# Rows of 1,088 instead of 1,056 elements in the weight tiles of a dense transformer block

## The chip, the cores and the metric

The kernel runs on one core of a Trainium2 chip. The metric is the device time of one execution in microseconds (us). Three runs of the kernel before took 1647.96, 1648.25 and 1648.37 us; the median is 1648.25 us.

## The reference

One layer of a streaming encoder on 256 frames of 2,048 features, all in float32:

```
h  = x + W_out( sum_b sigmoid(g_b) * W_branch_b( mixer_b( RMSNorm(x) ) ) )   # gated linear attention, gMLP
h  = h + W_down( relu(W_up RMSNorm(h))^2 )                                    # hidden size 8,192
y  = RMSNorm(h)
```

Nearly all the arithmetic is in products of a [256 x 2048] activation with 2,048 x 512 pieces of weight matrices: the input projection (14,352 columns), the two branch products, the output product, and the two products of the MLP.

## The kernel before

**Products.** `gemm` (line 185) multiplies 256 tokens by 2,048 rows and 512 columns of a weight matrix. It is called 72 times. 71 calls have 512 columns; one, the third, has 528 in two parts of 264. A call goes through its 2,048 rows in 8 blocks (`kb` 0 to 7) of 256 rows, two K-tiles of 128 rows each.

**Precision.** Each float32 operand is split into a high part in the format fp32r and a low part that holds the rest, and a product is made of three matmuls: high by high (line 197), low by high (line 198), high by low (line 199). A block of a call with 512 columns therefore has 2 K-tiles x 2 token tiles x 3 = 12 matmuls, and each has one K-tile of the activation, 128 x 128, as the stationary operand (read by the weight load, LDWEIGHTS) and 512 columns of the weights as the moving operand. So "weight load" in the profile's words reads the activation, and the matrix called weights here streams through. The moving operand of one matmul is 512 elements, 2,048 bytes, of each partition.

**Weight tiles.** `split_weights` (line 170) fetches a block: a load into a raw tile `w` issued on the queue of SyncE (line 178), a ScalarE copy that rounds it to the high part `wh` (line 179), and a VectorE subtraction that makes the low part `wl` (line 180). The three kinds of tile have 5, 4 and 4 buffers, which are taken in turn, one of each for a block. As every call has 8 blocks, the blocks with even `kb` use the buffers 0 and 2 of `wh` and `wl`, and those with odd `kb` the buffers 1 and 3, in every call.

**Activations.** The high and low parts of an activation, and most intermediate results, are in tiles of the pool `slots` (`slot`, 4 K-tiles x 256 tokens, 4,096 bytes of a partition; `pair` has the same size). K-tiles 0 and 1 of such a tile go with even `kb`, K-tiles 2 and 3 with odd `kb`. Smaller tiles `ev` and `bg` are in the pool `work`.

**Order.** The order of the work is the program's own; short steps (transposes, the small products of the mixers) are put between the blocks of the next product (`drain`). TensorE gets block after block without a gap as long as the buffers are filled in time.

**Places in SBUF.** The pools lie one behind the other in each partition: 16,384 bytes of scratch, 128 bytes of constants, the pool of constants and of the residual `h` up to byte 36,736, then the buffers of `w`, `wh` and `wl`, then `slots`, `work` and the small columns. A row of 1,056 float32 elements is 4,224 bytes, or 16.5 x 256; 36,736 is 143.5 x 256. In the built program the buffers begin here:

| tile | first byte of each buffer in a partition | remainder by 256 |
|---|---|---|
| `w` | 36,736, then every 4,224 | 128, 0, 128, 0, 128 |
| `wh` | 57,856, 62,080, 66,304, 70,528 | 0, 128, 0, 128 |
| `wl` | 74,752, 78,976, 83,200, 87,424 | 0, 128, 0, 128 |
| `slot`, `pair` | 91,648, then every 4,096 | 0 |
| `ev` / `bg` | 210,432 / 222,720, then every 2,048 | 0 |
| `h`, `ident` | 16,512, 33,408 | 128 |

A K-tile of a weight block begins 0 or 2,048 bytes into its buffer, and a stationary operand a multiple of 512 bytes into its `slot`, so the remainders are also those of the operands of the matmuls (in the calls with 512 columns).

Of the kernel before, what the change touches and what calls it, by code (L numbers as in the profile page):

```python
# [9 lines left out]
F32 = mybir.dt.float32  # L10
F32R = mybir.dt.float32r
# [24 lines left out]
C_GV = 8208  # L36
C_G = 10256

V_MLP, V_GLA, V_BA, V_BS = 0, 16, 20, 28
NVEC = 36  # L40


class Operand:
    """An activation with features on partitions, as high and low parts: tiles of 4 K-tiles."""

    def __init__(self):
        self.hi, self.lo = [], []
# [8 lines left out]
def block_kernel(  # L56
# [33 lines left out]
    def uid(s):  # L90
        count[0] += 1
        return f"{s}_{count[0]}"
# [2 lines left out]
        return slots.tile([P, 4, T], dt, tag="slot", name=uid("slot"))  # L95

    def pair_tile():
        """[128, 2, 512]: 512 features of both token tiles, tokens on partitions"""
        return slots.tile([P, NTT, CB], F32, tag="slot", name=uid("pair"))

    def flat(t):
# [14 lines left out]
    def cols(j, n=CB):  # L116
        return slice(j * n, (j + 1) * n)

    # As long as `in_order` is set, the steps on the way to the products keep their order.
    in_order = [True]  # L120

    def pin(ins):
        return tc.keep_in_program_order(ins) if in_order[0] else ins

    # Steps that need TensorE for a short time wait here, and run between the K-tiles of the
    # next large product, when what they read is long there.
    pending = deque()

    def drain(n=1):
        for _ in range(min(n, len(pending))):  # L130
            pending.popleft()()

    # ---- x, in blocks of 256 features; constants
    h = cpool.tile([P, NTT, D], F32, name="h")
    xv = x[0].rearrange("(t p) d -> p t d", p=P)

# [2 lines left out]
        nc.sync.dma_start(h[:, :, s], xv[:, :, s])  # L139

    def late(dst, src):
        """A load that must not run ahead of the weights'."""
        tc.keep_in_program_order(nc.scalar.dma_start(dst, src))

    load_x(0)
# [11 lines left out]
    nc.gpsimd.memset(starts.rearrange("p (c s) -> p c s", s=CHUNK)[:, :, 0:1], 0.0)  # L157

    def to_partitions(src, n, name):
        """[n, 128] -> [128, n]"""  # L160
        dst = cpool.tile([P, n], F32, name=name)
        tp = tr_ps()
        nc.tensor.transpose(tp[:, 0:n], src, ident[0:n, 0:n])
        pin(nc.vector.tensor_copy(dst, tp[:, 0:n]))
        return lambda i: dst[:, i : i + 1]

    mix_col = to_partitions(vec_n, KT, "mixw")

    # ---- shared steps
    def split_weights(src, by_k=False):  # L170
        """[128, nk, n] of DRAM -> its high and low parts in SBUF."""
        k, n = src.shape[1], src.shape[1] * src.shape[2]
        w = wpool.tile([P, 2 * 528], F32, tag="w", name=uid("w"), bufs=5)
        hi = wpool.tile([P, 2 * 528], F32R, tag="wh", name=uid("wh"), bufs=4)
        lo = wpool.tile([P, 2 * 528], F32R, tag="wl", name=uid("wl"), bufs=4)
        wv, hv, lv = [t[:, 0:n].rearrange("p (k n) -> p k n", k=k) for t in (w, hi, lo)]
        for s in [slice(i, i + 1) for i in range(k)] if by_k else [slice(0, k)]:
            nc.sync.dma_start(wv[:, s], src[:, s])  # L178
            pin(nc.scalar.copy(hv[:, s], wv[:, s]))  # L179
            pin(nc.vector.tensor_tensor(  # L180
                lv[:, s], wv[:, s], hv[:, s].bitcast(F32), op=ALU.subtract
            ))
        return hv, lv

    def gemm(a, w, c0, n=CB, parts=1, k0=0, after=None, split_tail=False):
        """256 tokens of a @ w[k0 : k0 + 2048, c0 : c0 + n]: PSUM tiles [part][token tile]."""
        ps = [[mm_ps() for _ in range(NTT)] for _ in range(parts)]
        m = n // parts
        held = []

        def products(kt, tt, hi, lo):
            ah, al = a.at(kt, tt)
            for i in range(parts):
                o = ps[i][tt][:, 0:m]
                wh = hi[:, kt % 2, cols(i, m)]
                wl = lo[:, kt % 2, cols(i, m)]
                pin(nc.tensor.matmul(o, lhsT=ah, rhs=wh, start=kt == 0, stop=False))  # L197
                pin(nc.tensor.matmul(o, lhsT=al, rhs=wh, start=False, stop=False))  # L198
                pin(nc.tensor.matmul(o, lhsT=ah, rhs=wl, start=False, stop=kt == KT - 1))  # L199

        for kb in range(KT // 2):
            r0 = k0 + kb * 2 * P
            hi, lo = split_weights(
                w[r0 : r0 + 2 * P, c0 : c0 + n].rearrange("(k p) n -> p k n", p=P),
                by_k=after is not None and kb == 0,
            )
            if after is not None:
                after(kb)
            if kb > 1 or kb == 1 and len(pending) > 6:
                drain()  # L210
            while a.ready < 2 * kb + 2:
                drain()
            if split_tail and kb >= KT // 2 - 3:
                held.append((kb, hi, lo))
                continue
            for kk in range(2):
                for tt in range(NTT):
                    products(2 * kb + kk, tt, hi, lo)
        if held:
            for tt in range(NTT):  # L220
                for kb, hi, lo in held:
                    for kk in range(2):
                        products(2 * kb + kk, tt, hi, lo)
        return ps

    def to_operand_pair(dst, src, scale=None):
        """Two K-tiles of dst from src[token tile] [128, 256], tokens on partitions."""
        kt0 = dst.ready
        if kt0 % 4 == 0:
            dst.hi.append(slot(F32R))  # L230
# [24 lines left out]
        dst.ready += 2  # L255

    def to_operand(dst, src, scale=None):
        """to_operand_pair of four K-tiles; TensorE's way is the shorter one."""
        for half in range(2):
            part = [src[:, tt, cols(half, 2 * P)] for tt in range(NTT)]  # L260
            pending.append(lambda part=part: to_operand_pair(dst, part, scale))

    def transpose_quadrants(dst, src, jm):
        """Rows 32 jm ... of dst [128, 4 K-tiles, 256 tokens], the transpose of a pair."""
        sv = src.rearrange("p t (k m b) -> p m k t b", m=4, b=32)
        dv = dst.rearrange("p k (t i b) -> p i k t b", t=NTT, b=32)
        for i in range(4):
            nc.vector.transpose(dv[cols(jm, 32), i], sv[cols(i, 32), jm])  # L268

    def to_operand_vector(dst, src, scale=None):  # L270
        """to_operand with VectorE's transposes, in blocks of 32."""
        tr = []

        def step(jm):
# [24 lines left out]
        pending.append(split)  # L299

    def rsqrt_of(sums, n, width=1):
        """(sums / n + eps) ** -0.5"""
        m = col(2)[:, 0:width]
        nc.vector.tensor_scalar(m, sums, 1.0 / n, EPS, op0=ALU.mult, op1=ALU.add)  # L304
        r = col(2)[:, 0:width]
        nc.gpsimd.tensor_tensor(r, m, mhalf[:, 0:width], op=ALU.pow)  # L306
        return r
# [12 lines left out]
        return r  # L320

    def scaled(ps, scale, func=AF.Copy):
        """func(ps * scale) of both token tiles, in SBUF."""
        res = pair_tile()
        for tt in range(NTT):
            nc.scalar.activation(res[:, tt, :], ps[tt], func, scale=scale[tt])  # L326
        return res

    # ---- the projection's operand; the rows' scale is applied behind the products
    wi = w_in[0]  # L330
    xT = Operand()
    xsq = [cpool.tile([P, 4], F32, name=f"xsq{tt}") for tt in range(NTT)]
# [12 lines left out]
            x_step(kb + 1)  # L345

    def transposed(ps, scale, into):
        """[256, 512] of the projection, with features on partitions."""
        sb = scaled(ps, scale)

        def step(jm):
# [16 lines left out]
        rstd_q.append(rq)  # L368
    transposed(ps, rstd, kT)

    # ---- constants that are needed later
    vec_m = cpool.tile([NVEC, P], F32, name="vec_m")
    for row, src in ((V_MLP, norm_mlp_w), (V_GLA, gla_norm_w), (V_BA, b_alpha)):
        n = src.shape[1] // P
        late(vec_m[row : row + n, :], src[0].rearrange("(a p) -> a p", p=P))
    late(vec_m[V_BS : V_BS + GROUPS, :], b_spatial[0])
    # w_alpha_up's rows as high, low and high parts, against the gate's high, high and low parts
    wal_in = flat(slot())[0 : 3 * RANK, :]
    for i in range(3):
        late(wal_in[i * RANK : (i + 1) * RANK, :], w_alpha_up[0])  # L380
# [36 lines left out]

        pending.append(step)

    # ---- mixer A: gated linear attention  # L420
    transposed(gemm(xT, wi, C_K + CB)[0], rstd, kT)
    for i in range(2):
        pending.append(lambda i=i: wal_step(i))

    # the last head's r and the gate's low-rank rows, in one product of two parts
    ps = gemm(xT, wi, C_R + 3 * CB, n=CB + RANK, parts=2)
    half = (CB + RANK) // 2
    glrT = cpool.tile([3 * RANK, T], F32R, name="glrT")
# [22 lines left out]

    pending.append(glr_step)

    # decays: features on partitions, tokens along the row
    E, decay, zs = [], [], []

    def z_step(b, pair):
# [12 lines left out]
                z[:, 2 * pair + i, :], zp[:, cols(i, T)], AF.Identity, bias=vcol(V_BA + dt)  # L470
            )

    # log sigmoid(z) = min(z, 0) - ln(1 + exp(-|z|)), and its sums along each chunk
    logs = []

    def log_step(b, func, **args):
        """One function for both halves in a row: a table of functions takes long to load."""
        if func is AF.Abs:
            logs.append(slot())
        src = zs[b] if func is AF.Abs else logs[b]  # L480
# [40 lines left out]
    for b in range(2):  # L521
        transposed(gemm(xT, wi, C_Q + b * CB)[0], rstd_q, qT)

    # scores[s, t] = sum_d q[t, d] k[s, d] exp(L[end of t's chunk, d] - L[s, d]), s on partitions
    S, scaled_qk = [], []

    def scale_step(b):
# [102 lines left out]

        pending.append(gate_step)

    # ---- gated merge of the branches
    mixed = []

    def merge(br, a):
# [20 lines left out]

    merge(0, oT)

    # ---- mixer B: gMLP spatial gating, a block of 128 frames per token tile  # L660
    ln = flat(slot())
    lnw, lnb = ln[:, 0:DG], ln[:, DG : 2 * DG]
    late(lnw, gmlp_ln_w[0].partition_broadcast(P))
# [53 lines left out]

    mT = merge(1, gT)

    # ---- the residual, and the MLP's operand  # L720
    hT = Operand()
    hsq = [cpool.tile([P, 4], F32, name=f"hsq{tt}") for tt in range(NTT)]
    for j in range(4):
# [6 lines left out]
            sum_squares(hsq[tt][:, j : j + 1], part[:, tt])  # L730
    rstd2 = [row_rstd(hsq[tt], f"rstd2{tt}") for tt in range(NTT)]

    # ---- MLP, in four stages of 2048 hidden features; the down product follows one stage behind
    def up(st, j, f):
        ps = gemm(hT, w_ff_up[0], st * D + j * CB)[0]
        a = scaled(ps, rstd2, AF.Relu)
# [22 lines left out]
                if j == 2:  # L759
                    rest.append(mean_square(fsq[tt][:, 0:3]))  # L760

    # ---- the final norm
    rest = []

    def mean_square(parts):
# [74 lines left out]
```

## Time and profile before

| | |
|---|---|
| median of three runs | 1648.25 us |
| span of the profiled execution, first to last instruction | 1647.4 us |
| TensorE (PE) matmul busy | 1630.6 us, 99% |
| weight loads (PEld) busy | 1332.3 us, 81% |
| VectorE (DVE) busy | 1130.2 us, 69% |
| ScalarE (ACT) busy | 753.4 us, 46% |
| DMA engines, mean share | 61% for the queue of the weight loads, 189 GB/s |

Engines: PE is TensorE's matmuls, PEld its weight loads, which run beside the matmuls. The duration shown for a matmul contains its passage through a pipeline, so two matmuls overlap; the distance from one start to the next is what a matmul costs. A number behind L is a line of the kernel.

### The profile page before, as it was taken

Reading aid. Unit: us, or ns where it says so; the run is one execution under the profiler, and the core shown is the slowest. Engines: PE = TensorE matmul, PEld = TensorE weight load, DVE = VectorE, ACT = ScalarE, POOL = GpSimd, SP = SyncE. Lnnn points to the kernel's source line nnn. Section 1 sums busy time; section 2 is a strip of 40 time slices with the busy share of each in tenths; the row PEclk is TensorE's granted clock in tenths of the full one; section 3 lists DMA queues with packets and bytes.
Section 4 is the critical chain, followed back from the end, with each engine's and each line's share of the span. In section 5 each row is a group of like instructions: output and inputs, shape, how many; then the busy total and the mean of one; then the engine's idle time right before and its main releaser. Section 6 shows DMA issues by size and latency. Waiting matters only on the chain.

```text
span 1647.4 us, 19352 instructions
## 1 busy us (share of the span) xinstructions
PE 1630.6 (99%) x7224; PEld 1332.3 (81%) x7224; DVE 1130.2 (69%) x1486; ACT 753.4 (46%) x864; POOL 23.3 (1%) x50
## 2 busy tenths in 40 slices
PE   8999999999999999999999999999999999999997
PEld 6878888888888888888888888888888888888886
DVE  5759576854555778877758778866666666666654
ACT  6475444544344444544445444444444444444443
POOL 0000000000000000000000000000000000000000
PEclk9999999999999999999999999999999999999999
DMA  7656566566676666666655656656556666656653
GB/s 242 205 164 179 153 181 188 179 207 197 198 209 182 190 181 185 186 204 197 196 184 185 195 169 194 207 190 188 183 182 192 193 196 199 192 190 189 214 191 114
DMA packets 163095, 311.75 MB, mean 189 GB/s; under 512 B 9812, under 2 KB 13192, under 8 KB 163000
## 3 DMA queue, kind: packets, MB, share of 16 engines
q1 hardware_dynamic: 160016, 306.35, 60.7%
q10 hardware_dynamic: 2984, 4.16, 0.8%
q8 instruction: 56, 0.92, 0.2%
q14 instruction: 39, 0.32, 0.1%
HBM read 308.37 MB, written 2.10 MB: 188 GB/s over the span
## 4 chain that ended last, share of the span: by engine, by line
PE 98%; DVE 1%; DMA 0%; issue 0%; ACT 0%; SPq 0%; POOL 0%; ACTq 0%; POOLq 0%; DVEq 0%
PE mm L199 32%; PE mm L197 32%; PE mm L198 32%; PE tr L561 1%; PE tr L609 0%; DVE slot L268 0%; PE tr L704 0%; PE tr L236 0%; DMA h<-in_x_dram 0%; DVE wl L180 0%; PE tr L464 0%; POOL col L306 0%; ACT wh L179 0%; SPq L178 0%; PE tr L412 0%
## 5 line engine op out<-in xcount | busy, mean ns | idle before, releaser
L180 DVE TENSOR_TENSOR wl<-w,wh 128x1024 fp32r<-128x1024 f32 (+2 forms) x577 | 700.8, 1222 | 450.5 <-ACT wh L179 445.6
L179 ACT CAST wh<-w 128x1024 fp32r<-128x1024 f32 (+2 forms) x577 | 602.7, 1046 | 763.0 <-PE mm L198 698.0
L199 PE MATMUL mm<-wl,slot 128*128 128x512 f32 (+1 forms) x2336 | 911.8, 390 | 1.7 <-DVE wl L180 1.7
L197 PE MATMUL mm<-wh,slot 128*128 128x512 f32 (+1 forms) x2336 | 913.3, 391 | 0.0
L198 PE MATMUL mm<-wh,slot 128*128 128x512 f32 (+1 forms) x2336 | 910.8, 390 | 0.0
L199 PEld LDWEIGHTS mm<-wl,slot 128*128 128x128 f32 x2336 | 439.0, 188 | 99.6 <-DVE wl L180 3.5
L198 PEld LDWEIGHTS mm<-wh,slot 128*128 128x128 f32 x2336 | 439.5, 188 | 96.0
L197 PEld LDWEIGHTS mm<-wh,slot 128*128 128x128 f32 x2336 | 439.6, 188 | 95.8
L268 DVE STREAM_TRANSPOSE slot<-pair 32x256 f32<-32x256 f32 x496 | 216.3, 436 | 8.3
L326 ACT ACTIVATE pair<-mm,rstd 128x512 f32<-128x512 f32 x58 | 39.8, 688 | 33.2 <-PE mm L199 33.0
L285 ACT CAST slot<-slot 128x1024 fp32r<-128x1024 f32 x23 | 24.3, 1055 | 28.3 <-DVE slot L268 28.3
L306 POOL TENSOR_TENSOR col<-col,mhalf 128x1 f32<-128x1 f32 (+1 forms) x20 | 17.9, 896 | 871.9 <-DVE col L304 579.6
L286 DVE TENSOR_TENSOR slot<-slot,slot 128x1024 fp32r<-128x1024 f32 x23 | 28.0, 1219 | 0.0
L752 DVE TENSOR_TENSOR h<-mm,h 128x512 f32<-128x512 f32 x32 | 22.1, 691 | 5.8 <-PE mm L199 5.5
L268 DVE STREAM_TRANSPOSE slot<-h 32x256 f32<-32x256 f32 x48 | 20.9, 436 | 0.9
L737 DVE TENSOR_TENSOR pair<-pair 128x1024 f32<-128x1024 f32 x16 | 19.5, 1218 | 0.0
L290 ACT ACTIVATE slot<-slot,vec 128x256 fp32r<-128x256 f32 x28 | 12.1, 499 | 15.3 <-DVE slot L268 15.3
L312 ACT ACTIVATE ev<-h 128x512 f32<-128x512 f32 x24 | 15.0, 628 | 8.1 <-DVE h L752 8.1
L251 DVE SCALAR_TENSOR_TENSOR slot<-tr,mixw,slot 128x256 fp32r<-128x256 f32 x16 | 7.0, 479 | 11.8 <-ACT slot L246 11.8
L707 DVE SCALAR_TENSOR_TENSOR pair<-tr,vec,pair 128x256 f32<-128x256 f32 x16 | 7.0, 479 | 7.5 <-PE tr L704 7.5
L291 DVE SCALAR_TENSOR_TENSOR slot<-slot,vec,slot 128x256 fp32r<-128x256 f32 x28 | 11.7, 478 | 0.0
L644 DVE SCALAR_TENSOR_TENSOR pair<-mm,rstd,bg 128x512 f32<-128x512 f32 x16 | 11.5, 749 | 0.1
(103 smaller groups left out, 260.5 us busy)
## 6 DMA issues: line engine op xcount, KB each, us to landing
w<-in_w_in_dram SPq DMA_DIRECT2D x215, 512.0 KB, 3.8
w<-in_w_ff_up_dram SPq DMA_DIRECT2D x128, 512.0 KB, 3.8
w<-in_w_ff_down_dram SPq DMA_DIRECT2D x128, 512.0 KB, 3.8
w<-in_w_branch_dram SPq DMA_DIRECT2D x64, 512.0 KB, 4.0
w<-in_w_out_dram SPq DMA_DIRECT2D x32, 512.0 KB, 4.0
w<-in_w_in_dram SPq DMA_DIRECT2D x8, 528.0 KB, 4.5
h<-in_x_dram SPq DMA_DIRECT2D x8, 256.0 KB, 7.4
bg<-in_b_gate_dram ACTq DMA_DIRECT2D x8, 256.0 KB, 4.7
```

The costliest lines, as they stand in the source:

```text
L179: pin(nc.scalar.copy(hv[:, s], wv[:, s]))
L180: pin(nc.vector.tensor_tensor(lv[:, s], wv[:, s], hv[:, s].bitcast(F32), op=ALU.subtract))
L197: pin(nc.tensor.matmul(o, lhsT=ah, rhs=wh, start=kt == 0, stop=False))
L198: pin(nc.tensor.matmul(o, lhsT=al, rhs=wh, start=False, stop=False))
L199: pin(nc.tensor.matmul(o, lhsT=ah, rhs=wl, start=False, stop=kt == KT - 1))
L268: nc.vector.transpose(dv[cols(jm, 32), i], sv[cols(i, 32), jm])
L285: nc.scalar.copy(hi, tr[0])
L286: nc.vector.tensor_tensor(lo, tr[0], hi.bitcast(F32), op=ALU.subtract)
L306: nc.gpsimd.tensor_tensor(r, m, mhalf[:, 0:width], op=ALU.pow)
L326: nc.scalar.activation(res[:, tt, :], ps[tt], func, scale=scale[tt])
L737: nc.vector.tensor_tensor(a, a, a, op=ALU.mult)
L752: nc.vector.tensor_tensor(part, ps[tt], part, op=ALU.add)
```

## The change

The row of the three weight tiles grows by 32 elements, or 128 bytes. The elements that are used stay the first 1,024 (or 1,056) of a row. Comments and docstrings are taken out as well, which makes no instruction.

```
+W_ROW = 1088
...
-        w = wpool.tile([P, 2 * 528], F32, tag="w", name=uid("w"), bufs=5)
-        hi = wpool.tile([P, 2 * 528], F32R, tag="wh", name=uid("wh"), bufs=4)
-        lo = wpool.tile([P, 2 * 528], F32R, tag="wl", name=uid("wl"), bufs=4)
+        w = wpool.tile([P, W_ROW], F32, tag="w", name=uid("w"), bufs=5)
+        hi = wpool.tile([P, W_ROW], F32R, tag="wh", name=uid("wh"), bufs=4)
+        lo = wpool.tile([P, W_ROW], F32R, tag="wl", name=uid("wl"), bufs=4)
```

No engine's list of instructions changes, neither in order nor in what it waits for nor in which buffer it uses. What changes are addresses. The new row is 4,352 bytes, 17 x 256, and what lies behind the weight tiles moves up by 13 x 128 = 1,664 bytes, 6.5 x 256:

| tile | first byte of each buffer, new | remainder by 256 |
|---|---|---|
| `w` | 36,736, then every 4,352 | 128 in all five |
| `wh` | 58,496, 62,848, 67,200, 71,552 | 128 in all four |
| `wl` | 75,904, 80,256, 84,608, 88,960 | 128 in all four |
| `slot`, `pair` | 93,312, then every 4,096 | 128 |
| `ev` / `bg` | 212,096 / 224,384, then every 2,048 | 128 |
| `h`, `ident` | as before | 128 |

[...]

## Rows read from the trace of the kernel before

**Rows 1.** The page's chain of waits, shares of the span by engine and by line.

```profile
PE 98%; DVE 1%; DMA 0%; issue 0%; ACT 0%; SPq 0%; POOL 0%; ACTq 0%; POOLq 0%; DVEq 0%
PE mm L199 32%; PE mm L197 32%; PE mm L198 32%; PE tr L561 1%; PE tr L609 0%; DVE slot L268 0%; PE tr L704 0%; PE tr L236 0%; DMA h<-in_x_dram 0%; DVE wl L180 0%; PE tr L464 0%; POOL col L306 0%; ACT wh L179 0%; SPq L178 0%; PE tr L412 0%
```

**Rows 2.** The core's span and TensorE's mean granted clock.

```profile
core 0: 1647.4 us, clock 0.998
```

**Rows 3.** Waits: who waited for whom: us in total, times, longest us.

```profile
ACT wh L179 <- PE mm L198: 698.0, 430, 2.5
...
ACT wh L179 <- DMA w<-in_w_in_dram: 6.3, 2, 5.5
...
ACT wh L179 <- DMA w<-in_w_ff_down_dram: 2.6, 1, 2.6
...
PE mm L199 <- DVE wl L180: 1.7, 2, 1.4
```

**Rows 4.** Timeline of PE, one call of `gemm`: start us, us, engine, line, operation.

```profile
1196.33 0.39 PE L197 MATMUL mm<-wh,slot 128*128 128x512 f32 x1
...
1199.06 0.40 PE L197 MATMUL mm<-wh,slot 128*128 128x512 f32 x1
...
1199.76 0.39 PE L197 MATMUL mm<-wh,slot 128*128 128x512 f32 x1
...
1201.62 0.39 PE L199 MATMUL mm<-wl,slot 128*128 128x512 f32 x1
1201.85 0.39 PE L197 MATMUL mm<-wh,slot 128*128 128x512 f32 x1
...
1202.55 0.39 PE L197 MATMUL mm<-wh,slot 128*128 128x512 f32 x1
...
1204.36 0.39 PE L199 MATMUL mm<-wl,slot 128*128 128x512 f32 x1
1204.59 0.40 PE L197 MATMUL mm<-wh,slot 128*128 128x512 f32 x1
...
1207.38 0.39 PE L197 MATMUL mm<-wh,slot 128*128 128x512 f32 x1
...
1210.11 0.40 PE L197 MATMUL mm<-wh,slot 128*128 128x512 f32 x1
```

**Rows 5.** Timeline of PE: products of the attention scores between two blocks.

```profile
223.45 1.52 PE L609 MATMUL tr<-ev,slot 128*128 128x512 f32 x6
224.81 0.40 PE L197 MATMUL mm<-wh,slot 128*128 128x512 f32 x1
```

**Rows 6.** Timeline of ACT in two blocks of that call.

```profile
1199.03 1.05 ACT L179 CAST wh<-w 128x1024 fp32r<-128x1024 f32 x1 [1.69 <-PE mm L198]
1201.82 1.05 ACT L179 CAST wh<-w 128x1024 fp32r<-128x1024 f32 x1 [1.74 <-PE mm L198]
```

**Rows 7.** Timeline of DVE in the same two blocks.

```profile
1200.11 1.23 DVE L180 TENSOR_TENSOR wl<-w,wh 128x1024 fp32r<-128x1024 f32 x1 [1.51 <-ACT wh L179]
1202.90 1.23 DVE L180 TENSOR_TENSOR wl<-w,wh 128x1024 fp32r<-128x1024 f32 x1 [1.56 <-ACT wh L179]
```

**Rows 8.** Timeline of PE: transposes of a `pair`.

```profile
846.28 0.60 PE L236 MATMUL tr<-ident,pair 128*128 128x128 f32 x4
846.63 0.48 PE L197 MATMUL mm<-wh,slot 128*128 128x512 f32 x1
```

**Rows 9.** Timeline of PE: transposes of the residual.

```profile
935.65 0.60 PE L236 MATMUL tr<-ident,h 128*128 128x128 f32 x4
936.01 0.48 PE L197 MATMUL mm<-wh,slot 128*128 128x512 f32 x1
```

**Rows 10.** Groups by line and shape: count, busy us, mean ns, idle before.

```profile
L199 PEld LDWEIGHTS mm<-wl,slot 128*128 128x128 f32 x2336 | 439.0, 188 | 99.6 <-DVE wl L180 3.5
...
L609 PE MATMUL tr<-ev,slot 128*128 128x512 f32 x36 | 9.5, 391 | 0.0
...
L704 PE MATMUL tr<-ev,wsT 128*128 128x256 f32 x48 | 7.0, 282 | 0.0
```

## The prediction

> **What bounds the kernel now.** I read the chain of waits first. [...] Then the waits: ScalarE spends 698 us waiting for TensorE to free a `wh` buffer, while TensorE waits for a low part twice, 1.7 us in all, and ScalarE for raw weights for 6.3 and 2.6 us [rows 3]. Everything that feeds TensorE is early. So the time is the number of matmuls times the distance between their starts, and an edit that moves only addresses can matter in one way: if an address changes that distance.
>
> Therefore the third view is the timeline of TensorE through one whole call, read for starts and not for durations. Blocks begin at 1196.33, 1199.06, 1201.85, 1204.59, 1207.38 and 1210.11 [rows 4]: 2.73, 2.79, 2.74, 2.79 and 2.73 us for the same 12 matmuls. This alternation runs through the program. Over the 527 blocks with 512 columns that have no other step of TensorE between them, the start-to-start times have a median of 2.735 us where `kb` is even (263 blocks) and 2.792 us where it is odd (264); [rows 4] shows five of them. Even blocks use the buffers of `wh` and `wl` that begin at a multiple of 256 bytes, odd blocks those that begin 128 bytes behind one. So the trace of before is already an experiment on the thing that is changed, and it says that a start at 128 costs about 0.056 us a block.
>
> Inside a block the difference is not even. In an odd block the matmuls from the fourth to the twelfth start 8 steps apart in 1.86 us (1199.76 to 1201.62), 0.233 each; in an even block in 1.81 us (1202.55 to 1204.36), 0.226 each [rows 4]. The first three steps take 0.70 us in both (1199.06 to 1199.76, 1201.85 to 1202.55): for three matmuls behind a switch the two kinds run alike, then each settles. Over all blocks the settled means are 0.2333 and 0.2268 us.
>
> **The change part by part.** What it says is that every buffer begins at a multiple of 256 bytes. What it does follows from the place of the first buffer: rows become a multiple of 256 long, but the raw tiles still begin at 36,736, which is 128 behind such a multiple, so now all 13 weight buffers have the remainder 128, and by the shift of 1,664 bytes `slot`, `pair`, `ev` and `bg` go from 0 to 128 as well. Should SBUF be counted from another base on the chip, nothing changes in the argument: buffer 0 of `wh`, of the cheap kind by measurement, moves by 640 bytes, 2.5 x 256, and buffer 0 of `wl` by 1,152, 4.5 x 256. Both land in the dear kind; the buffers 1 of the two move by 768 and 1,280, whole multiples of 256, and stay in it. Buffers 2 go with 0, buffers 3 with 1.
>
> *Moving operand.* 71 calls have 512 columns, 568 blocks. I leave out the 8 blocks of the first call, where TensorE waits for data. Of 560 blocks half are even. If each turned into an odd block as it stands: 280 x 0.056 = 15.7 us. But no block would follow one of the other kind any more, so the three matmuls behind a switch go too. A block of 12 settled odd steps is 12 x 0.2333 = 2.799 us. That makes 280 x (2.799 - 2.735) = 17.9 for the even ones and 280 x (2.799 - 2.792) = 2.0 for the odd ones, 19.9 us. The lower bound is 15.7. For the upper I let the three matmuls at a block's head keep the surcharge they show in even blocks, 0.70 - 3 x 0.2268 = 0.02 us at the view's resolution and 0.0145 over all blocks: 560 x 0.0145 = 8.1 more, 28 us. I take 19.9, because the settled steps are what the trace shows when nothing switches.
>
> *The other operands.* The stationary operands go from 0 to 128. No 512-column product of before has that, so bounds: nothing, as the load of 0.188 us [rows 10] fits inside a step of 0.227 to 0.233, and as four transposes whose stationary operand comes from `h` (remainder 128) take 0.36 us from the first to the next product and four from a `pair` (remainder 0) take 0.35 [rows 8, 9], where the loads follow each other directly; or, from above, the price of the moving operand once more, 0.0065 x 6,816 = 44 us. Below nothing is the first rival's case. The nearest rows are the transposes: I take nothing. The small products with `ev` as moving operand (36 of 512 columns, 48 of 256 [rows 10]) become dearer too: under 84 x 0.0065 = 0.5 us; I take 0.3.
>
> *The third call* (264 columns a part) has 8 blocks and moves by fractions of a microsecond: nothing.
>
> *ScalarE and VectorE.* The copy takes 1.05 us and the subtraction 1.23 us in an odd block and in an even one [rows 6, 7], so for these engines neither kind is dearer. The raw buffers go from three of five at 128 to five of five; the loads end so early that ScalarE waited for one only three times, 8.9 us in all [rows 3], and a slower TensorE gives them more room. What is late next is nothing: the bound stays TensorE, with every step a little longer.
>
> *Sum.* 1647.4 + 19.9 + 0.3 = 1667.6 us for a profiled execution. The median of the runs is 0.85 us above that span, so 1668.5 us for the median, 1.2% slower.
>
> **The rivals.**
>
> *The remainder matters only relative to the stationary operand: faster.* In before every stationary operand of the products begins at 0, so "moving operand at 128" and "the two 128 apart" are the same rows. If TensorE pays for reading two streams that are out of step, the change brings all of them into step, at 128 and 128. Then all 560 blocks become settled blocks of the cheap kind, 12 x 0.2268 = 2.722: 280 x (2.735 - 2.722) + 280 x (2.792 - 2.722) = 23 us, 1625 us, or 1632.5 if they only become even blocks as they stand. For it: in the rows of the products the two readings can't be told apart. Against it: the transposes, with `ident` at 128 as moving operand, cost the same with `h` (in step) and with `pair` (out of step) [rows 8, 9]; but these are short and may be limited by their loads. It decides if the blocks of the changed kernel start 2.72 to 2.74 us apart. [...]
>
> *The address is not the cause: same.* Even and odd `kb` differ also in the half of the `slot` that the stationary operand comes from. If that half were the cause, nothing moves: 1648.25 us. Against it stand the six score products of the second head's second token tile: their stationary operands are in the upper half of a `slot`, as in odd blocks, and their moving operands in `ev`, at a multiple of 256, and they take 1.36 us from 223.45 to 224.81, 0.227 each [rows 5], the cheap kind. What is left for this rival is some other thing that alternates with the blocks. [...]
>
> *The weight loads pay too: slower still.* With the upper bound of 44 us on top it would be 1712 us. A sign would be weight loads longer than 0.188 us.
>
> **How the numbers follow.** A measurement of this kernel can tell about 0.2%, 3.3 us, from no change. I give the main case 0.77, in its own range of 1663 to 1677; the in-step rival 0.11; no effect 0.08; the dearer weight loads 0.04. So faster 0.11, same 0.08, slower 0.81. The range reaches down over the case of no effect, to 1647, since the main case alone doesn't fill 8 in 10, and up to 1680, where the upper bound of the heads of blocks ends.
>
> **What would show it.** Right: starts of blocks 2.79 to 2.81 us apart for odd and even `kb` alike; settled steps of 0.233 everywhere; the copy at 1.05, the subtraction at 1.23 and the weight loads at 0.188 us as before; TensorE still on 98% or more of the chain, at the same clock. If the starts still alternate, the cause isn't the start address; if all are 2.72 to 2.74, it is the relative one; if they exceed 2.82, the stationary operand pays too. If the starts are 2.80 and the span hasn't grown, the time went into an idle stretch of TensorE that I haven't seen.

## Result and the profile after

The changed kernel takes 1625.92 us (median of 4 runs, 1625.57 to 1626.48) against 1648.31 us of the kernel before; the ratio is 0.9863, 95% interval 0.985 to 0.9875. It is 1.4% faster where 1.2% slower was forecast, and lies outside the range. One run below, of the kernel a quarter out of step, had a granted clock of 0.655 and took 2320.51 us; its comparison leaves it out. The span of the profiled execution fell by 23.3 us. In the new file every line number is 3 higher: lines 197, 198 and 199 are now 200, 201 and 202.

Span and granted clock of the core, which answer to [rows 2]:

```profile
core 0: 1624.1 us, clock 0.998
```

The chain of waits, shares by engine and by line, against [rows 1]:

```profile
PE 97%; DVE 1%; DMA 0%; issue 0%; ACT 0%; SPq 0%; POOL 0%; ACTq 0%; POOLq 0%; DVEq 0%
PE mm L200 32%; PE mm L202 32%; PE mm L201 32%; DVE slot L271 1%; PE tr L564 1%; DVE wl L183 1%; PE tr L612 1%; DMA h<-in_x_dram 0%; PE tr L707 0%; PE tr L239 0%; ACT wh L182 0%; PE tr L467 0%; POOL col L309 0%; SPq L181 0%; PE tr L415 0%
```

The waits (total us, times, longest us) against [rows 3]:

```profile
ACT wh L182 <- PE mm L201: 683.4, 434, 2.4
...
PE mm L202 <- DVE wl L183: 2.3, 4, 1.5
```

TensorE is still 97% of the chain, at the same clock, and the engines that feed it still wait for it. What changed stands in TensorE's timeline of the same call as [rows 4], the starts of its first blocks:

```profile
1179.99 0.39 PE L200 MATMUL mm<-wh,slot 128*128 128x512 f32 x1
...
1182.71 0.39 PE L200 MATMUL mm<-wh,slot 128*128 128x512 f32 x1
...
1185.43 0.39 PE L200 MATMUL mm<-wh,slot 128*128 128x512 f32 x1
...
1188.15 0.39 PE L200 MATMUL mm<-wh,slot 128*128 128x512 f32 x1
```

These blocks take 2.72 us each; 2.735 and 2.792 alternated before. Over the 527 undisturbed blocks (those with no small step of TensorE in between) the median is 2.720 us, 12 steps of 0.2267, the settled step of the even blocks of before. A call takes 21.76 us where it took 22.11. With 560 blocks the change of the mean from 2.7635 to 2.720 is 24.4 us, a little more than the span lost; some calls with small steps between their blocks gained less. The other engines' groups (busy us, mean ns, idle before) answer to [rows 6, 7, 10]:

```profile
L183 DVE TENSOR_TENSOR wl<-w,wh 128x1024 fp32r<-128x1024 f32 (+2 forms) x577 | 700.6, 1222 | 432.0 <-ACT wh L182 427.2
L182 ACT CAST wh<-w 128x1024 fp32r<-128x1024 f32 (+2 forms) x577 | 605.4, 1051 | 732.5 <-PE mm L201 683.4
...
L202 PEld LDWEIGHTS mm<-wl,slot 128*128 128x128 f32 x2336 | 438.5, 188 | 93.6 <-DVE wl L183 4.5
```

Subtraction, copy and weight load take what they took. So the gain lies in the distance between matmuls, although all moving operands now begin 128 bytes behind a multiple of 256, where the odd blocks of before were dear.

### The profile page after: what moved, and what is told of

The parts are those of the page before. It is cut to its first block, busy times and chain, and to the rows that moved or that the text cites. A ratio compares the mean times of both kernels' runs of the same rounds, so it can differ in the third digit from the quotient of the medians.

```text
span 1624.1 us, 19352 instructions
## 1 busy us (share of the span) xinstructions
PE 1606.1 (99%) x7224; PEld 1330.5 (82%) x7224; DVE 1128.0 (69%) x1486; ACT 755.9 (47%) x864; POOL 23.3 (1%) x50
## 4 chain that ended last, share of the span: by engine, by line
PE 97%; DVE 1%; DMA 0%; issue 0%; ACT 0%; SPq 0%; POOL 0%; ACTq 0%; POOLq 0%; DVEq 0%
PE mm L200 32%; PE mm L202 32%; PE mm L201 32%; DVE slot L271 1%; PE tr L564 1%; DVE wl L183 1%; PE tr L612 1%; DMA h<-in_x_dram 0%; PE tr L707 0%; PE tr L239 0%; ACT wh L182 0%; PE tr L467 0%; POOL col L309 0%; SPq L181 0%; PE tr L415 0%
## 5 line engine op out<-in xcount | busy, mean ns | idle before, releaser
L288 ACT CAST slot<-slot 128x1024 fp32r<-128x1024 f32 x23 | 24.3, 1056 | 32.3 <-DVE slot L271 32.3
L249 ACT ACTIVATE slot<-tr,mixw 128x256 fp32r<-128x256 f32 x16 | 6.7, 471 | 10.6 <-PE tr L239 10.6
```

What stands on the lines that cost most here:

```text
L288: nc.scalar.copy(hi, tr[0])
```

## Experiments

Theory A is the first rival of the prediction: a matmul costs more where its moving and its stationary operand begin at different remainders by 256. Theory B: all weight buffers have one remainder now, and that nothing alternates is what helps. Theory C: a stationary operand at 128 is cheap whatever the moving one is. "Gap" is an unused tile that only shifts what lies behind it. In step means that the two operands of a matmul have equal remainders by 256, out of step that they don't. A step is the distance from one matmul's start to the next. Where steps repeat in a fixed pattern, the pattern is here called a rhythm, and a settled step is the mean over it.

**Activations moved back, weights left (out of step).** The changed kernel with

```
+    gap = ctx.enter_context(tc.tile_pool(name="gap", bufs=1))
+    gap.tile([P, 32], F32, name="gap_s")
```

between the pools `wpool` and `slots`, 128 bytes:

> The changed kernel with 128 unused bytes between the weight tiles and the activations: weight buffers stay at remainder 128 by 256, activations go back to 0. Theory A (in step: a matmul costs more where its moving and its stationary operand begin 128 bytes apart by 256): every block settles at 12 x 0.2333 = 2.80 us, 1666 to 1670 us. Theory B (uniform: what helped is that all weight buffers have one remainder, so that nothing alternates): blocks at 2.72 us, 1626 us. Theory C (a stationary operand at 128 is cheap whatever the moving one is): stationary back at 0, moving at 128, dear as the odd blocks were, 1664 to 1670 us.

Measured: 1663.33 us (1662.70 to 1664.07), ratio to before 1.009 (1.0075 to 1.0105). Starts of blocks in the timeline of the same call:

```profile
1205.82 0.40 PE L202 MATMUL mm<-wh,slot 128*128 128x512 f32 x1
...
1208.61 0.39 PE L202 MATMUL mm<-wh,slot 128*128 128x512 f32 x1
...
1211.40 0.39 PE L202 MATMUL mm<-wh,slot 128*128 128x512 f32 x1
```

Blocks of 2.79 us, even and odd: nearly all undisturbed blocks take 2.78 to 2.80. With the same weight addresses as the changed kernel and the activations 128 bytes further, all of the gain is lost and 15 us more, 37 us in all. Theory B falls, as the weight buffers are uniform here. The time is 3 us under A's figure, because most blocks settle below 2.80; their median is 2.791.

**Only the activations moved.** The kernel before with the same gap:

> The kernel before with 128 unused bytes between the weight tiles and the activations: rows of 1,056 as before (remainders 0, 128, 0, 128), activations at 128 instead of 0. Theory A (in step): the alternation turns round, even blocks 2.79 us, odd blocks 2.735 us, and the time stays at 1648 us. Theory B (uniform): nothing changes, even 2.735, odd 2.79, 1648 us. Theory C (stationary at 128 is cheap): all blocks 2.72 us, 1626 us.

Measured: 1648.20 us, ratio 0.9998 (0.9988 to 1.0008). Starts of blocks `kb` 0 to 3 of that call:

```profile
1196.08 0.40 PE L199 MATMUL mm<-wh,slot 128*128 128x512 f32 x1
...
1198.87 0.39 PE L199 MATMUL mm<-wh,slot 128*128 128x512 f32 x1
...
1201.61 0.40 PE L199 MATMUL mm<-wh,slot 128*128 128x512 f32 x1
...
1204.40 0.39 PE L199 MATMUL mm<-wh,slot 128*128 128x512 f32 x1
```

The blocks take 2.79, 2.74 and 2.79 us: the alternation has turned round against [rows 4], with the weights where they were. Even blocks, moving operand at 0, are dear now, since the stationary one is at 128. Theory C falls, and so does every theory in which the place of the moving operand alone decides, the one of the forecast among them. The time can't tell this kernel from before; the timeline can.

**Everything at a multiple of 256.** The changed kernel with the gap ahead of the weight tiles, which makes true what the change says of itself:

```
+    gap = ctx.enter_context(tc.tile_pool(name="gap", bufs=1))
+    gap.tile([P, 32], F32, name="gap_w")
```

between the pools `cpool` and `wpool`, 128 bytes:

> The changed kernel with 128 unused bytes ahead of the weight tiles: every weight buffer and every activation begins at a multiple of 256, which is what the change says. Theories A and B: blocks at 2.72 us, 1626 us, no different from the changed kernel. Theory C, or any in which the remainder 128 itself is what helps: blocks of 2.735 us or more, 1632 us or more.

Measured: 1625.43 us (1625.01 to 1626.59), ratio 0.9861 (0.9846 to 0.9876); the median block takes 2.720 us. No different from the changed kernel: 0 and 0 is as good as 128 and 128.

**TensorE alone.** Rows of 48 matmuls, all reading one moving and one stationary tile (a second pair in bfloat16); nothing of the block is computed:

```
    def run(name, m, s, n=512, count=48, a=mov, b=sta):
        ...
        for i in range(count):
            m0 = m[i % len(m)]
            s0 = s[i % len(s)] + 128 * (i % 2)
            pin(nc.tensor.matmul(
                o[:, 0:n], lhsT=b[:, s0 : s0 + 128], rhs=a[:, m0 : m0 + n], start=True, stop=True
            ))
```

> None of the block is computed: TensorE alone runs rows of 48 matmuls of 512 columns, with moving and stationary operand begun at chosen bytes behind a multiple of 256; the distance between starts is read. If TensorE alone is the place (theory A): 0.227 us where the two are at the same remainder (0 and 0, 128 and 128, 64 and 64), 0.233 us where they are 128 apart, whichever of them is moved; for 16 to 224 bytes apart A says only 'not less than 0.227'. If the cost needs the other engines' reads and writes of SBUF, all rows take 0.227 us. With the two operands turning together, own pair in step: 0.227 if the pair of one matmul counts; if what counts is the moving operand against the weight load that runs beside it, which is the next matmul's, then that row is dear and the crossed one is cheap.

TensorE's timeline, one row a group (start us, us, operation, moving and stationary tile); a step is the distance to the next row's start divided by 48. Half is 128 bytes, A 16, B 32, C 64, D 96, F 192:

```profile
26.19 11.04 PE L110 MATMUL mZero_sZero<-mov,sta 128*128 128x512 f32 x48
37.07 11.35 PE L110 MATMUL mHalf_sZero<-mov,sta 128*128 128x512 f32 x48
48.26 11.36 PE L110 MATMUL mZero_sHalf<-mov,sta 128*128 128x512 f32 x48
59.46 11.06 PE L110 MATMUL mHalf_sHalf<-mov,sta 128*128 128x512 f32 x48
70.36 11.29 PE L110 MATMUL mA_sZero<-mov,sta 128*128 128x512 f32 x48
81.48 11.37 PE L110 MATMUL mB_sZero<-mov,sta 128*128 128x512 f32 x48
92.69 11.15 PE L110 MATMUL mC_sZero<-mov,sta 128*128 128x512 f32 x48
103.67 11.37 PE L110 MATMUL mD_sZero<-mov,sta 128*128 128x512 f32 x48
...
148.51 11.36 PE L110 MATMUL mZero_sC<-mov,sta 128*128 128x512 f32 x48
159.71 11.16 PE L110 MATMUL mZero_sF<-mov,sta 128*128 128x512 f32 x48
170.71 11.06 PE L110 MATMUL mC_sC<-mov,sta 128*128 128x512 f32 x48
181.61 11.30 PE L110 MATMUL mZero_sTurn<-mov,sta 128*128 128x512 f32 x48
...
225.80 5.92 PE L110 MATMUL short_mZero_sZero<-mov,sta 128*128 128x256 f32 x48
231.55 5.86 PE L110 MATMUL short_mHalf_sZero<-mov,sta 128*128 128x256 f32 x48
237.25 10.53 PE L110 MATMUL bf_mZero_sZero<-movh,stah 128*128 128x512 bf16 x48
247.62 10.52 PE L110 MATMUL bf_mHalf_sZero<-movh,stah 128*128 128x512 bf16 x48
257.98 10.52 PE L110 MATMUL bf_mHalf_sHalf<-movh,stah 128*128 128x512 bf16 x48
```

10.88 / 48 = 0.2267 us at 0 and 0 and 0.2271 at 128 and 128 (0.2267 once settled), 0.2331 and 0.2333 with one of them 128 off, whichever it is. The program gives the other engines nothing but one load, four copies and one store of the input, all issued ahead of the rows, and TensorE's first row, which waited for ScalarE's copy of `sta`, began at 10.51 us; so nothing here points to contention with ScalarE, VectorE or a transfer. The difference has a sign: with the moving operand 64 bytes on (mC_sZero) the settled step is 0.2289, with the stationary one 64 on (mZero_sC) 0.2333, and with it 192 on (mZero_sF), which by 256 is the moving one 64 on, 0.2289 again; both at 64 take 0.2267. So moving less stationary, by 256, sets the step. With 256 columns the surcharge is gone (0.1198 and 0.1188), and with bfloat16 there is none (10.37 / 48 = 0.216 in both). Of the rows in which both operands turn by 128 with every matmul, own pair in step took 0.2283 and the crossed pairing 0.2300, so neither reading of "pair" came out clean.

**A finer map of TensorE alone.** The same, with other differences, shorter rows and single matmuls out of step:

> None of the block is computed: TensorE alone, rows of 48 matmuls as in the first map. Differences of 4, 8, 12, 24, 48, 56, 72, 80, 176 and 240 bytes: theory A says nothing under 0.2267 us, so no layout is cheaper than in step; a step near bfloat16's 0.216 us at some difference would point to a better kernel. Differences of 256, 384 and 512 bytes: 0.2267, 0.2333 and 0.2267 us if the period is 256. Rows with one matmul of 16 out of step: if what clashes is the moving stream and the weight load that runs beside it (which is the next matmul's), then moving the stationary operand of one matmul disturbs the steps from one earlier than moving its moving operand; if the clash is within one matmul's own pair, both disturb from the same step. Shorter rows (448, 384 and 320 columns): the surcharge of 128 bytes stays 0.0067 us a step if it is paid once a matmul, and shrinks with the columns if it is paid along the stream; with 256 columns it was gone (0.1200 in step, 0.1186 out of step).

```profile
148.14 11.04 PE L110 MATMUL mFull<-mov,sta 128*128 128x512 f32 x48
159.02 11.35 PE L110 MATMUL mFullHalf<-mov,sta 128*128 128x512 f32 x48
170.21 11.06 PE L110 MATMUL mDouble<-mov,sta 128*128 128x512 f32 x48
181.11 11.04 PE L110 MATMUL pause<-mov,sta 128*128 128x512 f32 x48
```

Differences of 256, 384 and 512 bytes: 0.2267, 0.2331 and 0.2271 us. The price repeats after 256 bytes. Settled steps of both maps, stationary operand at 0:

```
bytes  0      4      8      12     16     24     32     48     56     64     72
us     0.2267 0.2367 0.2333 0.2289 0.2317 0.2333 0.2333 0.2300 0.2300 0.2289 0.2356
bytes  80     96     128    160    176    192    224    240    256    384    512
us     0.2311 0.2333 0.2333 0.2344 0.2311 0.2333 0.2333 0.2333 0.2267 0.2333 0.2267
```

Nothing in the map lies below 0.2267, so none of these layouts is better than in step. The surcharge of 128 bytes is smaller in shorter rows, though not evenly: 0.2026 to 0.2040 us at 448 columns, 0.1733 to 0.1760 at 384, 0.1467 both at 320. One stationary operand of 16 out of step lengthened two steps, the first of them one matmul early (0.233, 0.234); one moving operand lengthened its own step (0.234); both together, which keeps the own pair in step, disturbed 12 steps, again from one matmul early, and cost most (0.060 us).

**A quarter out of step.** The changed kernel with 192 bytes between weights and activations:

```
+    gap = ctx.enter_context(tc.tile_pool(name="gap", bufs=1))
+    gap.tile([P, 48], F32, name="gap_s")
```

> The changed kernel with 192 unused bytes ahead of the activations, which begin at remainder 64; the weight buffers stay at 128, so a moving operand begins 64 bytes behind its stationary one by 256. Theory A as mapped with TensorE alone (settled step 0.2289 us at a difference of 64, 0.2333 at 128, 0.2267 at 0): blocks of 2.747 us, 15 us over the changed kernel, 1641 us. If only the bit for 128 counts (a difference under 128 is free): 1626 us. If every difference costs alike: 1663 us, as with 128.

Measured: median 1645.37 us, ratio 0.9978 (0.9968 to 0.9988). Two stretches of the timeline of this one execution:

```profile
545.86 0.40 PE L202 MATMUL mm<-wh,slot 128*128 128x512 f32 x1
...
548.66 0.40 PE L202 MATMUL mm<-wh,slot 128*128 128x512 f32 x1
...
1194.87 0.39 PE L202 MATMUL mm<-wh,slot 128*128 128x512 f32 x1
...
1197.62 0.39 PE L202 MATMUL mm<-wh,slot 128*128 128x512 f32 x1
```

A block takes 2.747 us, as the map says, in 414 of the 527, and 2.800 us in most of the others. The dear ones (101) lie in one stretch, from 540 to 850 us. It begins behind six small products of TensorE and ends at transposes; three more interruptions by such products inside it changed nothing. 101 x 0.053 = 5 us is about what the time is over A's 1641 us. So out of step has more than one rhythm, and an interruption can change it.

**Only the low parts out of step.** The changed kernel with `wl` in a pool of its own behind a gap of 128 bytes, and another gap behind it:

```
...
-        lo = wpool.tile([P, W_ROW], F32R, tag="wl", name=uid("wl"), bufs=4)
+        lo = lpool.tile([P, W_ROW], F32R, tag="wl", name=uid("wl"), bufs=4)
```

> The changed kernel with the low parts of the weights alone set 128 bytes off (high parts and activations at 128, low parts at 0): every third matmul is out of step. If the price is paid by each such matmul by itself, and in full: 4 of 12 steps at 0.2333, blocks of 2.747 us, 1641 us. If the price needs a run of them to build up (the odd blocks of before began with three steps that were no dearer than those of even blocks), less: 1626 to 1635 us. If a switch itself costs (the even blocks of before paid 0.0145 us behind each switch), more: 1645 to 1660 us.

Measured: 1662.99 us, ratio 1.0085 (1.007 to 1.01): a third of the matmuls out of step costs as much as all of them. The timeline at one of the interruptions, first matmul of each three (line 205), and transposes (line 420):

```profile
483.21 0.39 PE L205 MATMUL mm<-wh,slot 128*128 128x512 f32 x1
...
483.89 0.39 PE L205 MATMUL mm<-wh,slot 128*128 128x512 f32 x1
...
484.58 0.39 PE L205 MATMUL mm<-wh,slot 128*128 128x512 f32 x1
...
488.49 0.60 PE L420 MATMUL tr<-ident,slot 128*128 128x128 f32 x4
...
492.42 0.39 PE L205 MATMUL mm<-wh,slot 128*128 128x512 f32 x1
...
493.12 0.39 PE L205 MATMUL mm<-wh,slot 128*128 128x512 f32 x1
```

Ahead of the transposes three steps take 0.687 us, behind them 0.70. Of the undisturbed blocks, 96 in one stretch from 196 us up to these transposes took 2.747 us, the price of four steps out of twelve, and 421 took 2.785 to 2.805. None of the three expectations had this: in one rhythm only the matmuls out of step are longer (steps of 0.226, 0.227 and 0.234 us), in the other all are (0.230, 0.236 and 0.234).

**What a switch costs.** TensorE alone again, with both operands turning by 128 bytes every 16 matmuls:

> None of the block is computed: TensorE alone, rows of 96 matmuls of 512 columns. In three rows both operands go from remainder 0 to 128 and back every 16 matmuls: together, the moving operand one matmul ahead, or one matmul behind. If the clash is within a matmul's own pair, 'together' runs at 0.2267 us throughout and the two others pay at the switches. If it is between the moving stream and the weight load beside it, the next matmul's, 'moving early' runs at 0.2267 throughout. If every change of remainder disturbs the rhythm by itself, all three pay, and the row that turns by 256 bytes, which changes the address alone, doesn't. Rows with every third or every sixth moving operand 128 off: if each pays for itself, 0.2289 and 0.2278 us a step on average; the kernel with the low parts off (a third) ran at 0.2333, so if that comes from TensorE alone, the row of thirds runs there too.

```profile
36.21 21.98 PE L110 MATMUL together<-mov,sta 128*128 128x512 f32 x96
58.03 11.05 PE L110 MATMUL rest_a<-mov,sta 128*128 128x512 f32 x48
68.91 22.18 PE L110 MATMUL movingEarly<-mov,sta 128*128 128x512 f32 x96
90.93 11.09 PE L110 MATMUL rest_b<-mov,sta 128*128 128x512 f32 x48
101.85 22.29 PE L110 MATMUL movingLate<-mov,sta 128*128 128x512 f32 x96
123.98 11.05 PE L110 MATMUL rest_c<-mov,sta 128*128 128x512 f32 x48
134.86 21.92 PE L110 MATMUL fullTurn<-mov,sta 128*128 128x512 f32 x96
156.62 11.04 PE L110 MATMUL rest_d<-mov,sta 128*128 128x512 f32 x48
167.50 22.14 PE L110 MATMUL third<-mov,sta 128*128 128x512 f32 x96
189.47 11.04 PE L110 MATMUL rest_e<-mov,sta 128*128 128x512 f32 x48
```

96 matmuls take 21.82 us turning together, 22.02 with the moving operand early, 22.13 with it late, and 21.76 turning by 256. So the five switches by 128 cost 0.06 us even in step, each two longer steps, and the pairing with the next matmul's load is worse than the own pair. The row of thirds takes 21.97 / 96 = 0.2289: from an undisturbed start each pays for itself. The dear rhythm of the kernel with the low parts out of step did not appear in this row. That it needs interruptions fits the places where it began and ended, but isn't shown: no run put small steps into rows of TensorE alone.

## Why the prediction was wrong

- *What bounds the kernel.* Right. With TensorE on 97% of the chain at a granted clock of 0.998, against 98% and 0.998 in [rows 1, 2], the time is matmuls times their distance, and the change moved that distance alone.
- *The place of the buffers.* Right as a fact: 1,088 brings all 13 buffers to the remainder 128, not 0. The difference between 128 and 0 doesn't matter, as the kernel with everything at 0 takes the same time (1625.43 against 1625.92 us).
- *Moving operand.* This is the step that failed: "Both land in the dear kind". I gave the price to the address of the moving operand. The trace of before held the stationary operand at 0 throughout, so its rows showed the price of a difference and could not say whose address makes it. Activations moved alone turned the alternation round, to 2.79, 2.74 and 2.79 us, which shows that the difference decides. The sum fits another layout than the changed kernel's: with the activations left at 0 the time was 1663.3 us, the low end of the main case's range and 5 us under the sum, as blocks settled at 2.79 and not at 12 x 0.2333 = 2.799.
- *The other operands.* "I take nothing" belongs to the same mistake: between weights at 128 with activations at 0 and the changed kernel, moving them by 128 took 37 us off. I chose by the transposes [rows 8, 9], which have 128 columns. With TensorE alone the surcharge of 128 bytes was already gone at 320 columns (0.1467 us both) and 256 (0.1198 in step, 0.1188 out of step), and the transposes of a `pair`, out of step before and in step after, take 0.35 to 0.36 us before and 0.35 after, so these rows could not decide it. The score products of [rows 5] became no dearer either: 1.36 us before and after.
- *The first rival.* It named what decides, the difference of the two addresses, and its figure of 1625 us and settled blocks of 2.722 us (measured: 1625.92 and 2.720) follow the prediction's own working. In the rows of the products it stood level with the forecast, so its chance of 0.11 was too low; nothing in the rows but the transposes stood against it, and those could not decide it. The runs with TensorE alone show that the two operands' addresses interact, by 0.0067 us a step (0.2333 us with the two 128 bytes apart, 0.2267 in step). The range left the case out.
- *The second rival.* It fell: neither the half of the `slot` nor anything else that alternates with the blocks is the cause, as even and odd blocks of the changed kernel both have a median of 2.720 us. The addresses are the cause: with TensorE alone, differences of 16, 32 and 64 bytes gave steps of 0.2317, 0.2333 and 0.2289 us against 0.2267.
- *The third rival.* It fell: weight loads stayed at 0.188 us, and blocks became shorter.
- *The three matmuls behind a switch.* Right that they go when nothing alternates: 2.720, not 2.735. With TensorE alone such a surcharge shows as well, for two or three steps behind a change of remainder: 96 matmuls took 21.82 us with five changes by 128 and 21.76 with none.
- *ScalarE and VectorE.* Right: 1.05 and 1.22 us as before.
- *Two roundings.* 84 x 0.0065 is 0.55 us, not under 0.5, and the upper bound of the heads of blocks ends at 1677, not 1680. Neither bears on the outcome.

What stays open is how TensorE reads its operands. Shown is that, with TensorE alone, the difference of the two addresses sets the settled step: 0.2267 us at 0, 256 and 512 bytes, 0.2333 at 128 and 384. Which matmul's stationary operand the moving one meets is not settled: over runs of 16 the own pair in step was cheapest (21.82 us against 22.02 and 22.13), yet a single matmul turned whole disturbed more steps (12) than one turned by half (1 or 2). Open too is why the price doesn't grow steadily with the difference, why it goes with short rows, and why a dear rhythm out of step stays until an interruption.

## What to carry to other kernels

Where TensorE is the bound and fp32r operands of 512 columns stream, look at distances between starts, grouped by buffer. A distance that alternates with the buffers of one tile, as 2.735 and 2.792 us did here, can be an address effect, and the trace may hold one operand fixed that the change will move. Give the moving and the stationary tiles starts with one remainder by 256 bytes and rows that are a multiple of 256 long, all of them: in step a matmul took 0.2267 us here, 128 bytes out of step 0.2333, and a third out of step cost as much as all (1663.0 and 1663.3 us). A layout that is half right may measure the same as the mirror image of it (1648.31 and 1648.20 us here), so read the timeline as well as the time.

## What the runs showed of the hardware

- Matmuls of TensorE in fp32r, 512 columns, each with its own weight load: 0.2267 us a step with both operands at one remainder by 256 bytes, 0.2289 to 0.2367 at the other differences tried, with TensorE alone; in bfloat16 no difference at 128 bytes, 0.216 us.
- Out of step the same layout ran in two rhythms in one execution, 2.747 and 2.800 us a block, and each change from one to the other fell on small steps of TensorE between blocks. In step, blocks came back to 2.720 after every interruption.
